# Plain fp32 products for 64 up blocks of a two-layer expert-retrieval kernel

## The chip, the cores and the metric

The kernel runs on one core of one Trainium2 chip. The metric is the device time of one execution in microseconds; smaller is better. Engines are named as in the profile: PE (matrix products; PEld its weight loads), DVE, ACT, POOL, and SP, which here only issues transfers.

## What is computed

A decoder trunk of two layers over 512 tokens of width 1024, in fp32. Layer 0 mixes tokens by sparse attention, layer 1 by a Mamba-2 scan; each adds a cross-attention into 256 memory tokens. After either mixer comes the part that the change touches, PEER: every token asks for experts by a product key, and each expert is one neuron.

```
q = (h @ w_q).reshape(b, s, 8, 2, 128)
scores = einsum('bshic,ikc->bshik', q, sub_keys)
top_s, top_i = top_k(scores, 16)
...
expert, gate = the best 16 of the 256 pairs, softmax
act = gelu(einsum('td,thkd->thk', xt, u[et]))
out = einsum('thk,thkd->td', act * gt, v[et])
```

There are 128 x 128 = 16384 experts, 8 heads and 16 experts a head, so a token uses 128 of them.

## The kernel before, in words

PE's fast product takes fp32r operands. To keep fp32 accuracy, `split` (L74 to L78) writes an operand as a sum hi + lo: ACT copies hi (L77), and DVE, or POOL by default in `wblock`, subtracts lo = src - hi (L78). `mm3` (L68 to L72) then makes three products: hi hi, hi lo, lo hi. The names w_raw, w_hi, w_lo are a weight block of 128x1024 and its parts; hT is the normed and transposed activation, hi and lo.

`peer` treats the four tiles of 128 tokens in two ways. Tile 0 is **gathered**: `gather_tile` fetches for each of the 128 slots one row of u, later one of v, for all 128 tokens (POOL's indirect transfers, L1087), and DVE multiplies and sums (L1093, L1104). Tiles 1 to 3, 384 tokens, are computed **densely** over all experts: an up block is 128 experts, `act = gelu(uT . hT)`, and a down block multiplies act with the gate matrix gt and adds `act^T . v` into six PSUM banks, acc. There are 128 up and 128 down blocks a layer.

The stages of a layer's `peer`:

- the norm with its transposes (`norm_T`, `transpose_o`), and the 16 w_q blocks with their scores (sc) and top-16 searches on DVE;
- for the tiles in the order 1, 2, 0, 3: `decode` (DVE), and for tiles 1 to 3 `gate_blocks`, which builds the gate matrices in 8 chunks of 16 tokens a tile: four DVE products of 128x2048 (tiles oh, L1067 to L1070), 32 PE products g (L1075), four ACT copies st (L1076). They go to DRAM (gd). Beside that the first SPILL = 32 up blocks run, whose act goes to DRAM too (ad);
- the 32 down blocks of the spilled blocks, with act_r read back;
- the ring: up block i and down block i - 8 in turn for the other 96 blocks, then the last 8 down blocks;
- the sums: x += acc for tiles 1 to 3 (L969), and for tile 0 the two halves of the gather's acc and x (L1106, L1107). Layer 1 is followed by the final norm.

RATE says how many rows of tile 0 are gathered for each down block: 0.7 in the spilled part, 2.75 in the ring, 1.1 at its end; 257 steps are needed. The order in which each engine's instructions stand is set by a scheduler when the program is built. It keeps the order of dependent work but moves independent work by its own estimates, within the pools' buffers: w_raw has 3, w_hi and w_lo 2, oh 9. An engine then keeps its order strictly. Buffers of the pool p_pre (the gates) and of p_v (down blocks and rows) share memory, so the second can be filled only as the first comes free.

Of the kernel before, what the change touches and what calls it, by code (L numbers as in the profile page):

```python
# [10 lines left out]
F32 = mybir.dt.float32  # L11
# [4 lines left out]
F16 = mybir.dt.float16  # L16
AF = mybir.ActivationFunctionType
# [5 lines left out]
D = 1024  # L23
S = 512
NT = 4
KC = D // 128
# [9 lines left out]
class Trunk:  # L36
# [116 lines left out]

    def norm_T(self, xs, x, hi, lo, parts=2):


        nc = self.nc
        with self.tc.high_priority(self.hp):
            for t, xt in enumerate(x):
                s = xs(t)  # L160
                r = self.tile_rstd(xt, s, parts)
                nc.vector.scalar_tensor_tensor(s, xt, r, self.grow, op0=OP.mult, op1=OP.mult)
                self.transpose_o(s, 0, KC, (hi, lo), t)

# [183 lines left out]

    def transpose_o(self, o, k0, k1, oT, t, k_src=None):

        nc = self.nc
        d = 0 if k_src is None else k_src - k0
        for k in range(k0, k1, 4):
            n = min(4, k1 - k)
            p = self.psum([128, 4, 128], "tr")
            for i in range(n):
                nc.tensor.transpose(p[:, i], o[:, (k + d + i) * 128:(k + d + i + 1) * 128], self.ident)
            sl = slice(t * 128, t * 128 + 128)
            self.split(oT[0][:, k:k + n, sl], oT[1][:, k:k + n, sl], p[:, :n])

    def out_proj(self, l, oT, order, banks):
# [467 lines left out]
    GS = 32768.0  # L829
    RATE = (0.7, 2.75, 1.1)  # L830

    def peer(self, l, banks):
        self.use_banks(tr=banks[:2], mm=banks[2:4], sc=banks[4:5], g=banks[6:])
        nc, tc, I = self.nc, self.tc, self.I
        ND = NT - 1
        NC = ND * 128 // self.CH
        ad = self.dram.tile([self.SPILL, 128, ND * 128], F32, name=f"ad{l}")
        gd = self.dram.tile([NC, 128, 128 * self.CH], F32, name=f"gd{l}")
        with ExitStack() as es:
            up = es.enter_context(tc.tile_pool(name="p_u", bufs=2))  # L840
            res = es.enter_context(tc.tile_pool(name="p_res", bufs=1))
            exi = res.tile([128, 128], I32, name="exi")
            gate0 = res.tile([128, 128], F32, name="gate0")
            h0 = res.tile([128, D], F32, name="h0")
            hT = self.hT
            with ExitStack() as e2:
                pre = e2.enter_context(tc.tile_pool(name="p_pre", bufs=1))
# [8 lines left out]
                nc.sync.dma_start(sk, I["sub_keys"][l])  # L856
                self.norm_T(lambda t: pre.tile([128, D], F32, tag="oh", name="xs", bufs=9) if t else h0,
                            [self.x[:, t] for t in range(NT)], hT[0], hT[1])
                self.load_gain(3 if l == 0 else 5)
# [20 lines left out]
                for t in self.ORDER:  # L880
                    e, g = self.decode(pre, iu[:, t], bv[:, t], bp[:, t])
                    if t:
                        self.gate_blocks(pre, e, g, gd, (t - 1) * 128 // self.CH)
                    else:
                        nc.vector.scalar_tensor_tensor(e[0], e[0], 128.0, e[1], op0=OP.mult, op1=OP.add)
                        nc.vector.tensor_copy(exi, e[0])
                        nc.vector.tensor_copy(gate0, g)
            vp = es.enter_context(tc.tile_pool(name="p_v", bufs=2))
            self.use_banks(acc0=banks[:2], acc1=banks[4:6], acc2=banks[6:], mm=banks[2:4],
                           up=banks[2:4] + banks[5:6])  # L890
            acc = [[self.psum([128, 512], f"acc{t}") for _ in range(2)] for t in range(ND)]
            G = self.gather_tile(l, vp, h0, exi, gate0)
            acts, last = {}, []

            def up_block(i):

                w = self.wblock(I["uT"][l, i], eng=nc.vector if i >= self.SPILL else None)
                p = self.psum([128, ND * 128], "mm" if i >= self.SPILL else "up")
                for k in range(KC):
                    self.mm3(p, (w[0][:, k], w[1][:, k]), (hT[0][:, k, 128:], hT[1][:, k, 128:]), k == 0, k == KC - 1)  # L900
                a = up.tile([128, ND * 128], F32, tag="act", name="act", bufs=self.RING)
                nc.scalar.activation(a, p, AF.Gelu)
                if i < self.SPILL:
                    nc.sync.dma_start(ad[i], a)
                else:
                    acts[i] = a

# [43 lines left out]

            for i in range(self.SPILL):
                up_block(i)
            for j in range(self.SPILL):
# [40 lines left out]
    def decode(self, pool, iu, bv, bp):  # L995


        nc = self.nc
# [14 lines left out]
        for i in range(2):  # L1013
# [6 lines left out]
            nc.vector.tensor_copy(rf, ru)  # L1020
            im = pool.tile(shp, F16, tag="oh", name="tk_im", bufs=9)
            nc.scalar.copy(im, ix4[:, :, i, :, None].to_broadcast(shp))
            oh = pool.tile(shp, F16, tag="oh", name="tk_oh", bufs=9)
            nc.vector.tensor_tensor(oh, rf[:, :, None, :].to_broadcast(shp),
# [17 lines left out]
    def gate_blocks(self, pool, e, gate, gd, c0):  # L1042
# [17 lines left out]
        for c in range(128 // B):  # L1060
# [3 lines left out]
            col = [sT[:, i, c * B:(c + 1) * B, None].to_broadcast(shp) for i in range(4)]  # L1064
            oh = [pool.tile([128, B, 128], F16, tag="oh", name="oh", bufs=9) for i in range(4)]
            o4 = [x.rearrange("p t (a b) -> p t a b", b=2) for x in oh]
# [142 lines left out]
```

## Time and profile before

| | before |
|---|---|
| median of 3 runs (lowest to highest) | 3251.77 us (3250.94 to 3254.98) |
| the profiled execution | 3256.72 us |
| its span, first to last instruction | 3254.9 us |
| mean granted PE clock | 0.971 of full speed |
| busy: PE, DVE, ACT, POOL | 3013.9, 2374.3, 1362.3, 1212.0 us |

A view with starts gives us from the span's start, then the duration. A line number such as L78 can be that of a helper, so the tile's name tells what it works on. A matmul's duration is longer than its step, since products are pipelined; the pace is read from one start to the next. What stands in brackets behind a row is how long the engine had been idle, and what released it. The granted clock is a share of 2.4 GHz.

### The profile page before, as it was taken

The numbers are of one execution on the slowest core, as the hardware profiler recorded it, in microseconds if no ns is written. First come the engines' busy times: TensorE is split into PE (matmuls) and PEld (weight loads), VectorE is DVE, ScalarE is ACT, GpSimd is POOL, SyncE is SP. The second block draws the span as 40 slices with busy tenths as digits, with TensorE's granted clock in tenths as the row PEclk, the third lists the DMA queues.
The fourth block names the chain that finished last, engine by engine and source line by source line (L and its number), as shares of the span: only waits on it lengthen the run. The fifth ranks groups of instructions, "written<-read, shape, count | busy, mean of one in ns | idle before, by whom it ended". The sixth has DMA issues, their size and how long they took to land.

```text
span 3254.9 us, 44982 instructions
## 1 busy us (share of the span) xinstructions
PE 3013.9 (93%) x16369; PEld 2671.7 (82%) x16374; DVE 2374.3 (73%) x4611; ACT 1362.3 (42%) x2053; POOL 1212.0 (37%) x763
## 2 busy tenths in 40 slices
PE   8899987778999999999999999778889999999998
PEld 7787776777899999999978777667679999999997
DVE  6964898836587777877767579885566777777775
ACT  5573346643333333333345533665323333333332
POOL 3212435431044345554213334445112434445540
PEclk9899999999999999999999999889999999999999
DMA  4211224488699989998521122455877999989982
GB/s 164 90 50 54 74 99 185 184 292 292 222 329 335 322 316 324 336 324 315 201 93 52 67 72 83 181 187 214 310 256 270 318 326 335 323 313 327 332 290 82
DMA packets 241495, 727.33 MB, mean 223 GB/s; under 512 B 22092, under 2 KB 92792, under 8 KB 238200
## 3 DMA queue, kind: packets, MB, share of 16 engines
q1 hardware_dynamic: 162288, 448.66, 38.4%
q0 software_dynamic: 73728, 268.47, 23.7%
q10 hardware_dynamic: 5256, 7.32, 0.8%
q8 instruction: 128, 2.10, 0.3%
q14 instruction: 95, 0.78, 0.1%
HBM read 658.29 MB, written 66.08 MB: 223 GB/s over the span
## 4 chain that ended last, share of the span: by engine, by line
PE 73%; DVE 12%; DMA 5%; ACT 5%; issue 4%; POOL 2%; SPq 0%; POOLq 0%; DVEq 0%; ACTq 0%
PE mm L70 11%; PE mm L72 11%; PE mm L71 11%; PE acc L71 10%; PE acc L70 10%; PE acc L72 10%; DMA act_r<-ad 4%; ACT st L1076 2%; POOL w_lo L78 1%; PE g L1075 1%; PE up L70 1%; PE up L72 1%; PE up L71 1%; DVE oh L1070 1%; ACT w_hi L77 1%
## 5 line engine op out<-in xcount | busy, mean ns | idle before, releaser
L77 ACT CAST w_hi<-w_raw 128x1024 fp32r<-128x1024 f32 (+2 forms) x353 | 366.1, 1037 | 777.5 <-PE mm L71 609.0
L72 PE MATMUL mm<-hT,w_lo 128*128 128x384 f32 (+2 forms) x1928 | 668.1, 347 | 9.2 <-POOL w_lo L78 9.2
L70 PE MATMUL mm<-hT,w_hi 128*128 128x384 f32 (+2 forms) x1928 | 669.0, 347 | 0.0
L78 POOL TENSOR_TENSOR w_lo<-w_raw,w_hi 128x1024 fp32r<-128x1024 f32 (+2 forms) x157 | 472.0, 3014 | 528.4 <-ACT w_hi L77 464.0
L71 PE MATMUL mm<-hT,w_hi 128*128 128x384 f32 (+2 forms) x1928 | 667.8, 346 | 0.0
L71 PE MATMUL acc<-v_lo,a_hi 128*128 128x512 f32 x1536 | 608.2, 396 | 36.0 <-DVE v_lo L78 36.0
L70 PE MATMUL acc<-v_hi,a_hi 128*128 128x512 f32 x1536 | 605.1, 394 | 9.4 <-ACT a_hi L77 9.4
L72 PE MATMUL acc<-v_hi,a_lo 128*128 128x512 f32 x1536 | 603.6, 393 | 0.0
L1087 POOL DMA_INDIRECT row<-in_u,exi x256 | 300.0, 1172 | 697.1 <-DVE junk L1093 687.8
L1087 POOL DMA_INDIRECT row<-in_v,exi x256 | 386.5, 1510 | 391.0 <-DVE acc L1104 302.0
L78 DVE TENSOR_TENSOR w_lo<-w_raw,w_hi 128x1024 fp32r<-128x1024 f32 (+1 forms) x196 | 240.1, 1225 | 388.8 <-ACT w_hi L77 388.8
L72 PEld LDWEIGHTS mm<-hT,w_lo 128*128 128x128 f32 x1928 | 364.2, 189 | 25.1 <-POOL w_lo L78 12.7
L70 PEld LDWEIGHTS mm<-hT,w_hi 128*128 128x128 f32 x1928 | 365.3, 190 | 21.0 <-ACT hT L77 0.4
L71 PEld LDWEIGHTS mm<-hT,w_hi 128*128 128x128 f32 x1928 | 364.5, 189 | 20.3 <-DVE hT L78 0.4
L78 DVE TENSOR_TENSOR v_lo<-v_raw,v_hi 128x1024 fp32r<-128x1024 f32 x256 | 312.4, 1220 | 90.3 <-ACT v_hi L77 89.5
L71 PEld LDWEIGHTS acc<-v_lo,a_hi 128*128 128x128 f32 x1536 | 292.2, 190 | 97.0 <-DVE v_lo L78 42.7
L70 PEld LDWEIGHTS acc<-v_hi,a_hi 128*128 128x128 f32 x1536 | 291.8, 190 | 68.0 <-ACT a_hi L77 10.4
L72 PEld LDWEIGHTS acc<-v_hi,a_lo 128*128 128x128 f32 x1536 | 292.1, 190 | 62.5 <-DVE a_lo L78 0.3
L1104 DVE SCALAR_TENSOR_TENSOR acc<-row,gact,acc 128x1024 f32<-128x1024 f32 x252 | 314.5, 1278 | 0.0
L1093 DVE SCALAR_TENSOR_TENSOR junk<-row,h 128x1024 bf16<-128x1024 f32 x256 | 311.6, 1217 | 0.5 <-DMA row<-in_u,exi 0.4
L77 ACT CAST a_hi<-act 128x384 fp32r<-128x384 f32 x192 | 98.8, 514 | 495.2 <-PE acc L71 484.4
L77 ACT CAST v_hi<-v_raw 128x1024 fp32r<-128x1024 f32 x256 | 268.0, 1047 | 30.5 <-DMA v_raw<-in_v 19.1
(352 smaller groups left out, 4543.4 us busy)
## 6 DMA issues: line engine op xcount, KB each, us to landing
w_raw<-in_uT SPq DMA_DIRECT2D x256, 512.0 KB
v_raw<-in_v SPq DMA_DIRECT2D x256, 512.0 KB
gd<-st SPq DMA_DIRECT2D x24, 2048.0 KB
gt<-gd SPq DMA_DIRECT2D x32, 1536.0 KB
w_raw<-in_w_q SPq DMA_DIRECT2D x32, 512.0 KB
ad<-act SPq DMA_DIRECT2D x64, 192.0 KB
act_r<-ad SPq DMA_DIRECT2D x64, 192.0 KB
w_raw<-in_w_o SPq DMA_DIRECT2D x16, 512.0 KB
```

Of the source, the lines that this page charges most:

```text
L70: mm(out, lhs[0], rhs[0], start=start, stop=False)
L71: mm(out, lhs[0], rhs[1], start=False, stop=False)
L72: mm(out, lhs[1], rhs[0], start=False, stop=stop)
L77: self.nc.scalar.copy(hi, src)
L78: return (eng or self.nc.vector).tensor_tensor(lo, src, hi.bitcast(F32), OP.subtract)
L1070: nc.vector.tensor_tensor(o4[2], o4[0], col[2], OP.mult)
L1075: nc.tensor.matmul(p[:, i], oh[1][:, q + i], oh[k][:, q + i], start=k == 2, stop=k == 3)
L1076: nc.scalar.mul(st[:, :, o + q:o + q + 4].rearrange("p i t -> p t i"), p, 1.0 / self.GS)
L1087: nc.gpsimd.indirect_dma_start(out=g, out_offset=None, in_=I[name], in_offset=bass.IndirectOffsetOnAxis(ap=exi[:, s:s + 1], axis=0))
L1093: nc.vector.scalar_tensor_tensor(j, g, 1.0, h, op0=OP.mult, op1=OP.mult, accum_out=act[:, s:s + 1])
L1104: nc.vector.scalar_tensor_tensor(a, g, act[:, s:s + 1], a, op0=OP.mult, op1=OP.add)
```

## The change

The 32 up blocks beside the gates take the raw weights and an unsplit fp32 copy hw of the normed, transposed tiles 1 to 3, and PE makes one plain fp32 product for each of a block's eight 128-row slices. hw is written by ACT in `transpose_o` from the same PSUM tile as hT. hw and the blocks' act_s lie in p_pre, oh goes from 9 buffers to 8, and the pool p_u of the ring's act is opened after p_pre is closed, not before. RATE becomes (0.6, 2.6, 1.1).

```diff
-    def transpose_o(self, o, k0, k1, oT, t, k_src=None):
+    def transpose_o(self, o, k0, k1, oT, t, k_src=None, whole=None):
...
             self.split(oT[0][:, k:k + n, sl], oT[1][:, k:k + n, sl], p[:, :n])
+            if whole is not None:
+                nc.scalar.copy(whole[:, k:k + n, t * 128 - 128:t * 128], p[:, :n])
...
-    RATE = (0.7, 2.75, 1.1)
+    RATE = (0.6, 2.6, 1.1)
...
-            up = es.enter_context(tc.tile_pool(name="p_u", bufs=2))
...
+                hw = pre.tile([128, KC, ND * 128], F32, name="hw")
+                self.norm_T(lambda t: pre.tile([128, D], F32, tag="oh", name="xs", bufs=8) if t else h0,
+                            [self.x[:, t] for t in range(NT)], hT[0], hT[1], whole=hw)
...
+                self.use_banks(up=banks[2:4] + banks[5:6])
+                for i in range(self.SPILL):
+                    w = self.wst.tile([128, 1072], F32, tag="w_raw", name="w_raw", bufs=3)[:, :D]
+                    w = w.rearrange("p (k c) -> p k c", k=KC)
+                    nc.sync.dma_start(w, I["uT"][l, i])
+                    p = self.psum([128, ND * 128], "up")
+                    for k in range(KC):
+                        nc.tensor.matmul(p, w[:, k], hw[:, k], start=k == 0, stop=k == KC - 1)
+                    a = pre.tile([128, ND * 128], F32, tag="act_s", name="act_s", bufs=3)
+                    nc.scalar.activation(a, p, AF.Gelu)
+                    nc.sync.dma_start(ad[i], a)
+            up = es.enter_context(tc.tile_pool(name="p_u", bufs=2))
...
             def up_block(i):
-
-                w = self.wblock(I["uT"][l, i], eng=nc.vector if i >= self.SPILL else None)
-                p = self.psum([128, ND * 128], "mm" if i >= self.SPILL else "up")
+                w = self.wblock(I["uT"][l, i], eng=nc.vector)
+                p = self.psum([128, ND * 128], "mm")
...
-            for i in range(self.SPILL):
-                up_block(i)
             for j in range(self.SPILL):
                 rows(down_block(j), self.RATE[0])
```

How the built order moves, at three places. First ACT beside the first gate chunks of layer 0, before:

```order
L1076 ACTIVATE st<-g 128x4x128 x8
L77 CAST w_hi<-w_raw 128x1024
L902 ACTIVATE act<-up 128x384
L1076 ACTIVATE st<-g 128x4x128 x4
L77 CAST w_hi<-w_raw 128x1024
L1076 ACTIVATE st<-g 128x4x128 x2
```

and now (line numbers of the changed file are larger by 7 here; act_s is the spilled block's act, tk_im a copy that `decode` needs):

```order
L900 ACTIVATE act_s<-up 128x384
L1083 ACTIVATE st<-g 128x4x128 x8
L900 ACTIVATE act_s<-up 128x384
L1083 ACTIVATE st<-g 128x4x128 x8
L1029 COPY tk_im<-tk_ix 128x2048 x2
L1083 ACTIVATE st<-g 128x4x128 x2
```

The w_hi casts are gone, a Gelu stands between two chunks, and both tk_im copies stand ahead of a tile's last four st. On PE 39 up products now stand ahead of the first gate product, and one or three (some 2.7 on average) between the halves and the chunks of a tile; 15 stand between tiles 1 and 2, and 29 between tiles 2 and 3.

Second PE, where the gates of layer 0 end. Before, 139 split up products followed the last gate product, and then the down blocks:

```order
L71 MATMUL up<-hT_88,w_hi 128x384
L72 MATMUL up<-hT_87,w_lo 128x384
L70 MATMUL acc_6067<-v_hi,a_hi 128x512
L71 MATMUL acc_6067<-v_lo,a_hi 128x512
L72 MATMUL acc_6067<-v_hi,a_lo 128x512
```

Now 87 plain ones follow it, and then products of the ring's up blocks (84 until the first acc):

```order
L1082 MATMUL g<-oh 128x128
L898 MATMUL up<-hw,w_raw 128x384 x87
L70 MATMUL mm<-hT_87,w_hi 128x384
L71 MATMUL mm<-hT_88,w_hi 128x384
L72 MATMUL mm<-hT_87,w_lo 128x384
```

The ring's products that stood behind the 576 spilled down products become 132 instead of 216.

Third DVE, at the end of layer 1. Before, the last v_lo is followed by the sums of tiles 1 to 3 alone:

```order
L78 TENSOR_TENSOR v_lo<-v_raw,v_hi 128x1024
L969 TENSOR_TENSOR x<-acc_19866,x 128x512
L969 TENSOR_TENSOR x<-acc_19867,x 128x512
L969 TENSOR_TENSOR x<-acc_19868,x 128x512
L149 SCALAR_TENSOR_TENSOR w_raw,nss<-x 128x512
```

and now the gather's last step and its sums come among them (L1113 and L1114 are the old L1106 and L1107, L976 the old L969):

```order
L1111 SCALAR_TENSOR_TENSOR acc<-row,gact,acc 128x1024
L976 TENSOR_TENSOR x<-acc_19688,x 128x512
L1113 TENSOR_TENSOR acc<-acc 128x1024
L976 TENSOR_TENSOR x<-acc_19689,x 128x512
L1114 TENSOR_TENSOR x<-x,acc 128x1024
L976 TENSOR_TENSOR x<-acc_19690,x 128x512
```

Tile 0's norm, which stood far ahead of the last down blocks, comes last of the four. On SP's queue the loads of gt and v stood between the last ad stores; now they come behind all of them.

## Rows read from the trace of the kernel before

**Rows 1.** The page, busy us, share of the span and instructions of each engine.

```profile
PE 3013.9 (93%) x16369; PEld 2671.7 (82%) x16374; DVE 2374.3 (73%) x4611; ACT 1362.3 (42%) x2053; POOL 1212.0 (37%) x763
```

**Rows 2.** Stretches: length, busy PE, PEld, DVE, ACT, POOL, clock, DMA share, GB/s.

```profile
431.80:704.30 272.50, 209.72 (x1554) 192.61 (x1552) 202.84 (x324) 166.39 (x190) 135.49 (x39) 0.91 0.51 187
704.30:866.00 161.70, 139.25 (x576) 111.50 (x577) 99.12 (x143) 50.18 (x69) 22.38 (x22) 0.96 0.84 290
866.00:1663.00 797.00, 797.00 (x4042) 726.83 (x4041) 605.30 (x749) 281.92 (x393) 322.02 (x233) 1.00 0.83 294
```

**Rows 3.** Waits from 431.8 to 704.3: total us, times, longest.

```profile
PE up L72 <- POOL w_lo L78: 30.6, 9, 7.7
...
DVE oh L1069 <- PE g L1075: 28.7, 5, 9.0
```

**Rows 4.** Groups from 430 to 720: busy us, mean ns of one, idle before.

```profile
L78 POOL TENSOR_TENSOR w_lo<-w_raw,w_hi 128x1024 fp32r<-128x1024 f32 x32 | 130.5, 4088 | 125.6 <-ACT w_hi L77 103.5 <-PE up L72 15.1 <-PE g L1075 6.9
...
L1022 ACT COPY tk_im<-tk_ix 128x2048 f16<-128x2048 f16 x8 | 15.0, 1907 | 7.9 <-DVE tk_ix L1001 7.9
```

**Rows 5.** Timeline of DVE and POOL beside the gates: start, us, operation.

```profile
458.08 3.45 DVE L1024 TENSOR_TENSOR tk_oh<-tk_rf,iorank 128x2048 f16<-128x2048 f16 x1
...
471.06 3.42 DVE L1070 TENSOR_TENSOR oh<-oh,sT 128x2048 f16<-128x2048 f16 x1
...
487.07 19.11 POOL L78 TENSOR_TENSOR w_lo<-w_raw,w_hi 128x1024 fp32r<-128x1024 f32 x2 [9.21 <-ACT w_hi L77]
...
510.20 1.23 DVE L1069 TENSOR_TENSOR oh<-oh,sT 128x2048 f16<-128x2048 f16 x1 [8.55 <-PE g L1075]
```

**Rows 6.** Timeline of PE: the first gate product, and one chunk.

```profile
474.53 1.05 PE L1075 MATMUL g<-oh 128*128 128x128 f16 x16 [1.15 <-DVE oh L1070]
...
639.59 1.07 PE L1075 MATMUL g<-oh 128*128 128x128 f16 x16
640.47 0.42 PE L72 MATMUL up<-hT,w_lo 128*128 128x384 f32 x1
641.37 0.61 PE L1075 MATMUL g<-oh 128*128 128x128 f16 x8 [0.48 <-ACT st L1076]
...
642.69 0.42 PE L70 MATMUL up<-hT,w_hi 128*128 128x384 f32 x1
642.95 0.33 PE L71 MATMUL up<-hT,w_hi 128*128 128x384 f32 x1
643.12 0.34 PE L72 MATMUL up<-hT,w_lo 128*128 128x384 f32 x1
```

**Rows 7.** Timeline of PE in layer 1: two plain fp32 products.

```profile
1752.95 0.81 PE L790 MATMUL mm<-state,ccT 128*128 128x384 f32 x2
1753.60 0.81 PE L799 MATMUL mm<-xe,btm 128*128 128x384 f32 x2
```

**Rows 8.** Timeline of SP's issues, DVE and PE where the gates end.

```profile
688.70 0.37 SPq L912 DMA_DIRECT2D gt<-gd  x1
...
696.95 0.44 SPq L917 DMA_DIRECT2D act_r<-ad  x1
...
706.96 0.56 DVE L925 TENSOR_TENSOR act_r<-act_r,gt 128x384 f32<-128x384 f32 x1 [1.17 <-DMA act_r<-ad]
...
708.12 0.80 PE L70 MATMUL acc<-v_hi,a_hi 128*128 128x512 f32 x1 [3.87 <-ACT a_hi L77]
```

**Rows 9.** Waits from 704.3 to 866.

```profile
DVE act_r L925 <- DMA act_r<-ad: 47.1, 22, 6.9
...
PE acc L71 <- DVE v_lo L78: 18.6, 8, 5.2
```

**Rows 10.** Timeline of ACT in the norm of layer 0.

```profile
317.25 0.59 ACT L77 CAST hT<-tr 128x512 fp32r<-128x512 f32 x1 [4.98 <-PE tr L357]
```

**Rows 11.** Timeline of DVE near the end of layer 0's down blocks.

```profile
1595.61 1.22 DVE L1107 TENSOR_TENSOR x<-x,acc 128x1024 f32<-128x1024 f32 x1
...
1613.66 1.28 DVE L162 SCALAR_TENSOR_TENSOR w_raw<-x,rs_r,grow 128x1024 f32<-128x1024 f32 x1
```

More of the change, by code (lines that the diff above doesn't have):

```diff
@@ L152, in tile_rstd, with norm_T @@
         return self.rstd(ss[:, 0:1], D, 1)
-    def norm_T(self, xs, x, hi, lo, parts=2):
+    def norm_T(self, xs, x, hi, lo, parts=2, whole=None):
         nc = self.nc
@@ L162, in norm_T @@
                 nc.vector.scalar_tensor_tensor(s, xt, r, self.grow, op0=OP.mult, op1=OP.mult)
-                self.transpose_o(s, 0, KC, (hi, lo), t)
+                self.transpose_o(s, 0, KC, (hi, lo), t, whole=whole if t else None)
     def wblock(self, src, shape=(128, KC, 128), eng=None):
@@ L856, in peer @@
                 nc.sync.dma_start(sk, I["sub_keys"][l])
-                self.norm_T(lambda t: pre.tile([128, D], F32, tag="oh", name="xs", bufs=9) if t else h0,
-                            [self.x[:, t] for t in range(NT)], hT[0], hT[1])
+                hw = pre.tile([128, KC, ND * 128], F32, name="hw")
+                self.norm_T(lambda t: pre.tile([128, D], F32, tag="oh", name="xs", bufs=8) if t else h0,
+                            [self.x[:, t] for t in range(NT)], hT[0], hT[1], whole=hw)
                 self.load_gain(3 if l == 0 else 5)
@@ L887, in peer @@
                         nc.vector.tensor_copy(gate0, g)
+                self.use_banks(up=banks[2:4] + banks[5:6])
[10 more added lines that the diff above has]
+            up = es.enter_context(tc.tile_pool(name="p_u", bufs=2))
             vp = es.enter_context(tc.tile_pool(name="p_v", bufs=2))
-            self.use_banks(acc0=banks[:2], acc1=banks[4:6], acc2=banks[6:], mm=banks[2:4],
-                           up=banks[2:4] + banks[5:6])
+            self.use_banks(acc0=banks[:2], acc1=banks[4:6], acc2=banks[6:], mm=banks[2:4])
             acc = [[self.psum([128, 512], f"acc{t}") for _ in range(2)] for t in range(ND)]
@@ L895, in up_block @@
             def up_block(i):
-                w = self.wblock(I["uT"][l, i], eng=nc.vector if i >= self.SPILL else None)
-                p = self.psum([128, ND * 128], "mm" if i >= self.SPILL else "up")
+                w = self.wblock(I["uT"][l, i], eng=nc.vector)
+                p = self.psum([128, ND * 128], "mm")
                 for k in range(KC):
                     self.mm3(p, (w[0][:, k], w[1][:, k]), (hT[0][:, k, 128:], hT[1][:, k, 128:]), k == 0, k == KC - 1)
[L901 to L906, printed above, removed]
+                acts[i] = up.tile([128, ND * 128], F32, tag="act", name="act", bufs=self.RING)
+                nc.scalar.activation(acts[i], p, AF.Gelu)
             def down_block(j):
@@ L1020, in decode @@
             nc.vector.tensor_copy(rf, ru)
-            im = pool.tile(shp, F16, tag="oh", name="tk_im", bufs=9)
+            im = pool.tile(shp, F16, tag="oh", name="tk_im", bufs=8)
             nc.scalar.copy(im, ix4[:, :, i, :, None].to_broadcast(shp))
-            oh = pool.tile(shp, F16, tag="oh", name="tk_oh", bufs=9)
+            oh = pool.tile(shp, F16, tag="oh", name="tk_oh", bufs=8)
             nc.vector.tensor_tensor(oh, rf[:, :, None, :].to_broadcast(shp),
@@ L1064, in gate_blocks @@
             col = [sT[:, i, c * B:(c + 1) * B, None].to_broadcast(shp) for i in range(4)]
-            oh = [pool.tile([128, B, 128], F16, tag="oh", name="oh", bufs=9) for i in range(4)]
+            oh = [pool.tile([128, B, 128], F16, tag="oh", name="oh", bufs=8) for i in range(4)]
             o4 = [x.rearrange("p t (a b) -> p t a b", b=2) for x in oh]
```

## The prediction

> **What bounds the kernel now.** I began with the busy shares. PE is busy for 93% of the span, DVE for 73%, POOL for 37% [rows 1]. Such a share is an average over stages with different limits, so the table of stretches comes next [rows 2]. From 866 to 1663 PE is busy for 797.00 of 797.00 us at clock 1.00: there only fewer products could save time, and the change leaves those products as they are. Two other stretches are looser. From 431.8 to 704.3 the gate matrices and the 32 spilled up blocks run side by side: PE 209.7 of 272.5 us at clock 0.91, DVE 202.8. From 704.3 to 866 the 32 spilled down blocks run. Layer 1 runs the same code with other weights, so I take its saving alike.
>
> In the first stretch the waits tell who ends last [rows 3]: PE waited 30.6 us for POOL's w_lo, DVE 28.7 us for PE's gate products. POOL's w_lo takes 4088 ns on average [rows 4]; two in succession took 19.11 us, between 487.07 and 506.2, while DVE ran its fp16 products without a gap, and DVE then stood 8.55 us until PE had come past the late weights [rows 5]. It works the other way as well: an L1024 of DVE took 3.45 us and an L1070 3.42 us beside a w_lo on POOL, where the same size takes 1.23 us undisturbed [rows 5]. So POOL's splitting holds up PE and DVE, and the engines wait in a ring.
>
> **What the change removes.** Per layer 32 w_hi on ACT, 32 w_lo on POOL and 768 products of 384 columns at 0.174 us, the step from 642.95 to 643.12 [rows 6]: 24 a block, 4.2 us. POOL is left with nothing in this stage, so both kinds of hold-up go.
>
> **What it adds, on PE.** 256 plain fp32 products of 384 columns. Two such products stand back to back in the Mamba layer: L790 starts at 1752.95 and L799 at 1753.60, each in two passes [rows 7]. So one costs 0.65 us, a block 5.2 us against 4.2: 256 x 0.65 = 166.4 us instead of 133.6. The Trainium skill, "TensorE: Matmul & The Clock Gate", section Back-to-back issue gap, gives N/2.4 + 2.5 ns: for two passes of 768 that is an estimate of 0.645 us, and the stage would be 1.3 us shorter a layer. By the same rule one of the old products would take 162.5 ns; the row has 174, and the row decides.
>
> **The new stage, by PE's order.** PE keeps its written order, so I add up that order from 431.8.
> - 24 gate chunks. A chunk from its first product at 639.59 to the next up product at 642.69 takes 3.1 us, of which the waits for ACT's st are part [rows 6]. In the new order one fp32 product stands inside each chunk, where 0.9 us are free (640.47 to 641.37), so 24 of the 256 cost nothing as long as st sets the pace. 24 x 3.1 = 74.4.
> - The other 232 products: 232 x 0.65 = 150.8.
> - The four score products of 128 columns, a third of 0.65 each: 1.
> - The start: after 39 up products PE is ready at 458.2. The first gate product came at 474.5 before [rows 6]. Three DVE operations that POOL held up by 2.2 us each lie before it (two of them in [rows 5]), so it can now come at 467.9: 9.7 us of waiting.
> - ACT's two tk_im copies ahead of the last st of a tile (1.9 us each [rows 4]) delay the last chunk by about 2.5 us, twice: 5. Gelu between two st, some 12 times 0.2: 2.
>
> Together 242.9, so the last up product ends at about 675 instead of 704.25 (708.12 less the 3.87 of waiting [rows 8]): **30 us a layer saved**. DVE does not hold this up. Undisturbed, a chunk is four operations of 1.2 us there, 4.9 at most, against PE's 3.1 + 2.7 x 0.65 = 4.9 on average. With 8 oh buffers instead of 9 a chunk's second product (not its third) waits for PE, and DVE has some 3 us in hand; I cost it at nothing, and if it fails it costs about 0.4 us a chunk, 10 us a layer.
>
> **Handing over.** Before, PE stood 3.87 us between the last up and the first acc product [rows 8]. gt was issued at 688.70, act_r at 696.95, and the first multiplication started at 706.96: 10 us behind act_r, 18 behind gt. Now gt, v and act_r all come behind the last ad store, about 3 us after the end, so the first acc product can come 15 to 22 us after it. In between stand 84 ring products that came later before: 84 x 0.174 = 14.7 us. I take 3 us idle, as against 3.9: -1. If the cover is gone, the price is 8.
>
> **Down blocks.** 576 products of 512 columns, at 512/384 of 0.174 = 0.23 us, are 132.5 us; the stretch took 161.7 [rows 2]. PE waited 18.6 us there for v_lo, DVE 47.1 us for act_r [rows 9]. RATE takes 3 of 22 gathered rows away, 1.6 MB, and some two ring weights are loaded earlier: 2.6 MB of 47, at 290 GB/s 9 us of transfer. The bounds are 0 (what is late is one load, not the sum) and -9; I take **-4 a layer**. The Trainium skill, "SBUF — State Buffer", section A bandwidth-pool intuition that's wrong, gives a core some 358 GB/s of HBM: by that the 47 MB need an estimated 131 us, less than PE's 132.5, and the saving would be 0. No row here shows that ceiling; the mean of 290 [rows 2] stands below it.
>
> **The copy hw.** Six ACT copies of 128x512 a layer; the alike hT cast takes 0.59 us [rows 10]. They stand between casts for which PE waits, but ACT has pauses there. +1 a layer, bounds 0 and 3.5.
>
> **The ends of the layers.** With RATE 2.6 the gathering lasts until the last down block. Before, its sums (1.22 us each) were done at 1596.8 and tile 0's norm at 1614.9, both beside the down products [rows 11]. Now they stand between and behind the last x additions on DVE. In layer 1 two sums of 1.2, a square over half a tile (half a sum: 0.6), a norm of 1.28 and small steps come on top of DVE's closing work, less about 1 us that PE's last products cover: +5. In layer 0 tile 0's transposes and 24 short products that filled PE at the change of layers come later: +4. Bounds +3 and +7 each.
>
> **Sum.** 2 x (-30 - 1 - 4 + 1) + 9 = -59 us. The profiled execution took 3256.7 us, 1.8 outside its span of 3254.9; it lies 4.9 above the median of the runs, 3251.8. So 3251.8 - 59 = 3192.8, rounded to **3193 us**.
>
> **Rivals.**
> - *More*: nothing waits in the new stage. Then PE needs 166.4 + 24 x 1.76 (16 gate products in 0.88 us [rows 6]) + 1 = 209.6 us, 33 less than I count: 3193 - 2 x 33 = 3127. For it: POOL is out. Against it: the st of ACT remain, and the first gate matrix has to wait for DVE's decoding.
> - *Less*: a chunk takes 3.6 us instead of 3.1 (an ACT step of some 0.5 us between two st, an estimate from st's steps of 0.9 [rows 6]), 12 us a layer, the hand-over costs 4 more, and fewer rows give nothing: 3193 + 2 x 20 = 3233. For it: act_r was the late load throughout [rows 9].
> - *Slower*: the clock. The plain fp32 products of [rows 7] stand two in a row among split products, at full pace. Now 87 fp32 products stand in a row. If PE were granted the lower of its two levels (1.2 instead of 2.4 GHz) in them, each would take 1.3 us: 87 x 0.65 = 56.6 more a layer, 3193 + 113 = 3306. It decides from about 45 such products a layer (2 x 45 x 0.65 = 59). Against it: the stage's mean of 0.91 came with waits of up to 7.7 us [rows 3], and the new order has fewer.
> - *It does not overlap*: PE waits for raw weights, since SP's queue holds them behind gd and ad stores. The order issues a weight two blocks, 10 us, ahead; I give it little. If the 145 products between first and last gate matrix (232 less 87) lost half their cover, some 47 us a layer: 3193 + 94 = 3287.
>
> **How the numbers follow.** Forecast 0.70, with a range of its own from 3166 to 3214; more 0.06; less 0.17; the clock 0.05; no overlap 0.02. A measurement here can tell a difference from about 0.2%, 6.5 us. Forecast, more and nearly all of less are faster by more than that: 0.91. Same 0.03, out of the weaker end of less; slower 0.06. The range of 8 in 10 runs from 3162 to 3230: it takes in the forecast's own bounds and the nearer half of less, and leaves out more and the clock.
>
> **What would show it.** Right: no PE wait on POOL in the stage, 0.65 us from one up product to the next, DVE's 128x2048 products all at 1.22 us, the last up near 675, the first acc some 17 us behind it. The layers' ends about 4 us longer. Wrong: a granted clock near 0.5 in the row of 87, chunks of over 5.5 us, or a first acc over 23 us behind the last up.

## The result: 51.6 us faster, and the profile after

The changed kernel takes **3200.31 us** (median of 4 runs, 3199.93 to 3203.8), the kernel before 3251.86. The ratio is 0.9842, 95% interval 0.9825 to 0.9859. The forecast was 3193 us, in a range from 3162 to 3230. The profiled execution took 3199.93 us, with a span of 3198.1; it lies 56.8 us under the profiled one of before, for which the sum of the forecast was -59.

The page of the changed kernel, busy us, share of the span and instructions of the engines, against [rows 1]:

```profile
PE 3042.7 (95%) x15862; PEld 2570.8 (80%) x15862; DVE 2303.8 (72%) x4611; ACT 1305.1 (41%) x2001; POOL 953.0 (30%) x699
```

PE is busy 29 us longer with 507 instructions fewer, in a span that is 57 us shorter. POOL lost 259 us. Where the time went is read from the stretches between the same events as in [rows 2]: first up product, last up product, first acc product, first ring product behind the spilled down blocks, last acc product of layer 0, first z product of layer 1 (z is a product of its mixer), and the end. From the last up to the first acc product is called the hand-over here; the second stretch of [rows 2] held it, 3.8 us, together with 157.9 us of spilled down blocks. Stretches of the changed kernel: length, busy PE, PEld, DVE, ACT, POOL, clock, DMA share, GB/s.

```profile
431.80:669.57 237.77, 221.69 (x1299) 141.25 (x1297) 168.73 (x325) 137.17 (x161) 1.13 (x2) 0.99 0.56 203
669.57:689.52 19.95, 15.13 (x87) 14.71 (x85) 4.88 (x5) 5.91 (x9) 5.82 (x5) 1.00 0.90 305
689.52:846.06 156.54, 143.05 (x576) 114.85 (x577) 95.38 (x139) 47.59 (x66) 18.70 (x19) 0.92 0.80 278
846.06:1627.35 781.29, 781.29 (x3949) 711.24 (x3947) 597.38 (x727) 274.47 (x380) 322.35 (x234) 1.00 0.85 300
1627.35:1654.37 27.02, 19.11 (x129) 18.30 (x129) 17.76 (x51) 10.81 (x21) 2.90 (x7) 0.81 0.35 104
...
2245.14:2397.28 152.14, 139.95 (x577) 112.70 (x578) 94.90 (x139) 47.57 (x66) 19.81 (x19) 0.94 0.82 284
...
3178.54:3198.10 19.56, 0.15 (x1) 0.00 (x0) 11.61 (x39) 1.74 (x6) 3.73 (x4) 0.57 0.26 107
```

And the stretch of the kernel before that answers to the end of layer 0:

```profile
1662.90:1678.82 15.92, 15.14 (x122) 14.49 (x121) 11.65 (x32) 8.26 (x15) 1.40 (x5) 1.00 0.57 177
```

Set against each other, in us, layer 0 and layer 1 (changes from before to after; in brackets the lengths):

| step | forecast per layer | layer 0 | layer 1 |
|---|---|---|---|
| first to last up product | -30 | -34.7 (272.5 to 237.8) | -33.4 (272.5 to 239.1) |
| last up to first acc, less 84 products of 0.176 moved there | -1 | +1.3 (3.9 to 19.95) | +0.1 (5.6 to 20.5) |
| spilled down blocks | -4 | -1.4 (157.9 to 156.5) | -7.7 (159.8 to 152.1) |
| ring, less the same 84 products | 0 | -0.8 | +0.1 |
| the copy hw | +1 | 0.0 | +1.2 |
| end of the layer | +4, +5 | +11.1 (15.9 to 27.0) | +7.3 (12.3 to 19.6) |

The columns add up to -24.5 and -32.4, or -56.9. **The gate stage** gave 8 us more than forecast, **the ends** took 9.4 us more.

In the gate stage PE no longer waits for POOL. Ahead of the first gate product, at 466.9, it stands 7.0 us for DVE's decoding. What is left of its waits from there on, in us, times, longest:

```profile
PE g L1082 <- ACT st L1083: 8.4, 26, 0.8
```

That answers to 30.6 us on POOL's w_lo in [rows 3]. A chunk on PE, and the run of plain fp32 products behind the gates (one row: start, us, operation, count of passes):

```profile
476.45 1.06 PE L1082 MATMUL g<-oh 128*128 128x128 f16 x16
477.35 0.86 PE L898 MATMUL up<-hw,w_raw 128*128 128x384 f32 x2
478.24 0.61 PE L1082 MATMUL g<-oh 128*128 128x128 f16 x8
...
479.57 2.15 PE L898 MATMUL up<-hw,w_raw 128*128 128x384 f32 x6
...
614.07 55.63 PE L898 MATMUL up<-hw,w_raw 128*128 128x384 f32 x172
```

From 476.45 to 479.57 a chunk takes 3.1 us, as forecast. In the last row 172 passes lie in 55.63 us; one pass alone takes 0.486, so the step is (55.63 - 0.49) / 171 = 0.3225 us, or 0.645 for a product. The stretch of that run shows the clock, at 1.00 throughout:

```profile
613.86:669.57 55.71, 55.71 (x175) 32.79 (x174) 1.23 (x1) 8.06 (x14) 0.00 (x0) 1.00 0.54 181
```

The prediction's estimate of 0.645, worked out from the formula in the Trainium skill, "TensorE: Matmul & The Clock Gate", section Back-to-back issue gap, agrees with it; the 768 columns a pass were put in by the prediction, that section does not give them.

DVE's groups beside the gates, in the changed kernel and in the one before (busy us, mean ns of one, idle before):

```profile
L1075 DVE TENSOR_TENSOR oh<-iokey,sT 128x2048 f16<-128x2048 f16 x24 | 29.3, 1220 | 0.2
```

```profile
L1070 DVE TENSOR_TENSOR oh<-oh,sT 128x2048 f16<-128x2048 f16 x24 | 35.8, 1490 | 0.0
```

The mean of 1490 ns was a mixture of 1.22 us and some of up to 3.4; now the means of all four oh operations are 1219 or 1220 ns, and of the 28.7 us in which DVE waited for gate products [rows 3] 0.9 is left.

### The profile page after: what moved, and what is told of

It reads as the page before. It is cut to its first block, busy times and chain, and to the rows that moved or that the text cites. A ratio compares the mean times of both kernels' runs of the same rounds, so it can differ in the third digit from the quotient of the medians.

```text
span 3198.1 us, 43835 instructions
## 1 busy us (share of the span) xinstructions
PE 3042.7 (95%) x15862; PEld 2570.8 (80%) x15862; DVE 2303.8 (72%) x4611; ACT 1305.1 (41%) x2001; POOL 953.0 (30%) x699
## 4 chain that ended last, share of the span: by engine, by line
PE 75%; DVE 12%; DMA 5%; ACT 5%; issue 2%; POOL 1%; SPq 0%; POOLq 0%; ACTq 0%; DVEq 0%
PE acc L71 10%; PE acc L70 10%; PE acc L72 10%; PE mm L70 10%; PE mm L71 10%; PE mm L72 10%; PE up L898 8%; DMA act_r<-ad 3%; ACT st L1083 3%; PE g L1082 1%; DVE tk_s L982 1%; DMA gt<-gd 1%; DVE tki L985 1%; DVE tki L984 1%; PE po L597 1%
## 5 line engine op out<-in xcount | busy, mean ns | idle before, releaser
L77 ACT CAST w_hi<-w_raw 128x1024 fp32r<-128x1024 f32 (+2 forms) x289 | 298.7, 1034 | 712.8 <-PE mm L71 599.5
L70 PEld LDWEIGHTS mm<-hT,w_hi 128*128 128x128 f32 x1928 | 364.5, 189 | 22.1 <-ACT hT L77 1.4
L898 PE MATMUL up<-hw,w_raw 128*128 128x384 f32 x1024 | 358.1, 496 | 0.0
L1100 DVE SCALAR_TENSOR_TENSOR junk<-row,h 128x1024 bf16<-128x1024 f32 x256 | 312.0, 1219 | 2.1 <-DMA row<-in_u,exi 2.0
L78 POOL TENSOR_TENSOR w_lo<-w_raw,w_hi 128x1024 fp32r<-128x1024 f32 (+3 forms) x93 | 213.0, 2299 | 265.4 <-ACT w_hi L77 245.2
```

The lines of the kernel that those rows point to most:

```text
L70: mm(out, lhs[0], rhs[0], start=start, stop=False)
L77: self.nc.scalar.copy(hi, src)
L78: return (eng or self.nc.vector).tensor_tensor(lo, src, hi.bitcast(F32), OP.subtract)
L898: nc.tensor.matmul(p, w[:, k], hw[:, k], start=k == 0, stop=k == KC - 1)
L1100: nc.vector.scalar_tensor_tensor(j, g, 1.0, h, op0=OP.mult, op1=OP.mult, accum_out=act[:, s:s + 1])
```

## The hand-over and the end of a layer in the trace after

The hand-over in layer 0, in SP's issues, then DVE and PE:

```profile
670.63 0.33 SPq L901 DMA_DIRECT2D ad<-act_s  x1
...
674.38 0.38 SPq L921 DMA_DIRECT2D gt<-gd  x1
...
675.66 1.04 SPq L926 DMA_DIRECT2D act_r<-ad  x1
```

```profile
688.32 0.56 DVE L934 TENSOR_TENSOR act_r<-act_r,gt 128x384 f32<-128x384 f32 x1 [7.75 <-DMA v_raw<-in_v]
```

```profile
689.52 0.57 PE L70 MATMUL acc<-v_hi,a_hi 128*128 128x512 f32 x1 [4.82 <-issue]
```

act_r is issued 5 us behind the last store and the first multiplication starts 12.7 us later, so the first acc product comes 20 us behind the last up product. The 84 ring products that stand between them keep PE busy for 15.1 of these. DVE and ACT stand for the loads here, and PE once those products are done, while the DMA engines are nearly full: share 0.90 and 305 GB/s in the stretch.

The end of layer 0, on PE and on DVE:

```profile
1627.12 0.39 PE L72 MATMUL acc<-v_hi,a_lo 128*128 128x512 f32 x1
1633.58 1.94 PE L357 MATMUL tr<-ident,w_raw 128*128 128x128 f32 x8 [6.08 <-DVE rs_t L94]
```

```profile
1623.31 1.22 DVE L1113 TENSOR_TENSOR acc<-acc 128x1024 f32<-128x1024 f32 x1
...
1632.16 1.28 DVE L162 SCALAR_TENSOR_TENSOR w_raw<-x,rs_r,grow 128x1024 f32<-128x1024 f32 x1
```

The sums L1113 and L1114 stand among the last x additions now; the norm of tile 0, L162, is done at 1633.4, where it was done at 1614.9 before, 48 us ahead of the end of the down products [rows 11]. PE, which found tile 0 ready in the kernel before, stands 6.08 us here and 1.80 four microseconds later. What follows is slower too: the stretch from the first transpose on, two short products in it, and two such products of the kernel before.

```profile
1633.58:1640.00 6.42, 4.62 (x21) 4.11 (x21) 6.16 (x11) 3.33 (x6) 0.00 (x0) 0.50 0.04 14
```

```profile
1641.04 0.43 PE L72 MATMUL mm<-w_hi,hT 128*128 128x268 f32 x1
1641.26 0.42 PE L70 MATMUL mm<-w_hi,hT 128*128 128x268 f32 x1
```

```profile
1663.02 0.29 PE L71 MATMUL mm<-w_lo,hT 128*128 128x268 f32 x1
1663.15 0.28 PE L72 MATMUL mm<-w_hi,hT 128*128 128x268 f32 x1
```

They step by 0.22 us instead of 0.13. The stretch from 1627.35 to 1654.37 has a mean clock of 0.81, against 1.00 before: after it had stood, PE ran at the lower of its two levels, 0.50 from 1633.58 to 1640. Of the 11.1 us, 7.1 are idle time (7.9 against 0.8) and 4.0 are busy time (19.1 against 15.1), of which tile 0's eight transposes, which lay in the ring before, are some 1.8 at this clock.

The end of layer 1 is another case, since no PE product follows there: of its 7.3 us 5.4 are DVE's, busy for 11.6 us behind the last acc product instead of 6.25, and the rest is standing in the chain of the last norm.

## The experiments

Theory: POOL's splitting and DVE's fp16 products hold each other up, PE waits for both, and the change frees all three. Rivals: the gain comes from the blocks' new place in the program, or only from PE's own wait for w_lo. A second question was what the new rates do, a third what the plain fp32 products cost where nothing hides them.

**Split again, at the new place.** In the loop over spilled blocks; the copy hw goes as well:

```
-  nc.sync.dma_start(w, I["uT"][l, i])
+  w = self.wblock(I["uT"][l, i])
...
   for k in range(KC):
-      nc.tensor.matmul(p, w[:, k], hw[:, k], start=k == 0, stop=k == KC - 1)
+      self.mm3(p, (w[0][:, k], w[1][:, k]), (hT[0][:, k, 128:], hT[1][:, k, 128:]), k == 0, k == KC - 1)
```

> The changed kernel with split up blocks again: w_hi on ACT, w_lo on POOL, three products, no copy hw; place, pools, 8 oh buffers and rates as in the change. Theory (POOL's splitting holds up DVE and PE): the stage from 431.8 goes back to about 272 us, so the last up product ends near 704 instead of 669.6, and the time is about 3200 + 2 x 33 = 3266 us, 3255 to 3275. Rival (the gain came from the place of the blocks in the program and their pools): the stage stays under 250 us, 3200 to 3224 us.

Measured: 3261.58 us, ratio to the kernel before 1.0019 (1.0009 to 1.0029). The stage, and PE's and DVE's waits in it:

```profile
428.70:697.80 269.10, 205.85 (x1555) 188.53 (x1554) 204.11 (x325) 166.85 (x192) 125.64 (x34) 0.92 0.50 180
```

```profile
PE up L72 <- POOL w_lo L78: 30.1, 9, 6.6
DVE oh L1072 <- PE g L1079: 28.3, 5, 9.0
```

Both waits are back as they were in [rows 3], and the stage is 31 us longer than in the changed kernel, 29 in layer 1. It is 3.4 us shorter than in the kernel before, so the new place, the pools and the eighth oh buffer can be the source of 3 to 4 us of the gain there, no more. The rest sits in the way the blocks are computed.

**POOL alone.** Behind each gelu a subtraction on POOL that nobody reads.

```
-  nc.scalar.activation(a, p, AF.Gelu)
+  nc.scalar.activation(a, p, AF.Gelu, accum_out=pace[:, i:i + 1])
   nc.sync.dma_start(ad[i], a)
+  lo = self.wst.tile([128, 1072], F32R, tag="w_lo", name="w_lo", bufs=2)[:, :D]
+  nc.gpsimd.tensor_tensor(lo.rearrange("p (k c) -> p k c", k=KC), hw[:, :, :128],
+                          pace[:, i:i + 1, None].to_broadcast([128, KC, 128]), OP.subtract)
```

> The changed kernel, and behind each of the 32 gelus a subtraction of 128x1024 on POOL whose result nobody reads (it writes a w_lo buffer, as POOL did before). PE waits for nothing new. Theory A (POOL and DVE hold each other up): DVE's 128x2048 fp16 products go from 1.22 us on average to 1.6 or more, POOL's subtractions to about 4 us, and the stage grows by 15 to 40 us a layer: about 3250 us, 3230 to 3280. Theory B (what was saved is PE's own wait for the late w_lo): DVE's products may slow, the stage grows by less than 4 us a layer, 3200 to 3208 us.

Measured: 3248.73 us, ratio 0.9984 (0.9974 to 0.9994): 48 us of the 51.6 are gone again by the medians, 46 by the ratios. The stage in layer 0, PE's waits for DVE, DVE's and POOL's groups in it, and a piece of POOL's and DVE's timelines:

```profile
430.60:691.20 260.60, 229.17 (x1300) 144.00 (x1298) 196.55 (x325) 139.87 (x192) 111.98 (x33) 0.95 0.51 183
```

```profile
PE tr L1058 <- DVE tk_e L1041: 19.0, 3, 10.4
...
PE g L1086 <- DVE oh L1081: 3.2, 4, 1.1
```

```profile
L1079 DVE TENSOR_TENSOR oh<-iokey,sT 128x2048 f16<-128x2048 f16 x24 | 32.6, 1357 | 0.0
```

```profile
L904 POOL TENSOR_TENSOR w_lo<-hw,pace 128x1024 fp32r<-128x1024 f32 x32 | 112.8, 3532 | 137.5 <-ACT act_s L901 137.5
```

```profile
468.20 2.53 POOL L904 TENSOR_TENSOR w_lo<-hw,pace 128x1024 fp32r<-128x1024 f32 x1 [10.57 <-ACT act_s L901]
473.76 2.07 POOL L904 TENSOR_TENSOR w_lo<-hw,pace 128x1024 fp32r<-128x1024 f32 x1 [3.03 <-ACT act_s L901]
...
486.48 19.57 POOL L904 TENSOR_TENSOR w_lo<-hw,pace 128x1024 fp32r<-128x1024 f32 x1 [10.65 <-ACT act_s L901]
...
506.00 1.89 POOL L904 TENSOR_TENSOR w_lo<-hw,pace 128x1024 fp32r<-128x1024 f32 x1
```

```profile
468.89 2.92 DVE L1078 TENSOR_TENSOR oh<-iokey,sT 128x2048 f16<-128x2048 f16 x1
...
474.00 2.91 DVE L1081 TENSOR_TENSOR oh<-oh,sT 128x2048 f16<-128x2048 f16 x1
```

The stage is 23 us longer than in the changed kernel, 21 in layer 1, though no engine reads what POOL makes; theory B, with less than 4, falls. DVE is busy 196.6 us instead of 168.7 with as many instructions, and the mean of 1357 ns falls short of the 1.6 us that were expected. PE feels it through DVE: it stands 31.4 us instead of 16.1, and what is new are the waits for DVE's decoding (19.0 instead of 7.0) and for its oh (3.2 instead of none). The other 7.5 us are busy time, 229.2 instead of 221.7, at a mean clock of 0.95 instead of 0.99. The edit also puts 31 short readings of a sum on ACT, 0.2 us each; PE's wait for ACT's st is as it was, 8.5 us against 8.4.

The timelines show the lock itself: the two subtractions that start at 468.20 and 473.76 take some 2 us, and the DVE product beside each takes 2.9 instead of 1.22. The one that starts at 486.48 takes 19.57 us, while DVE, up to 504.07, starts an fp16 product every 1.13 us; the next takes 1.89 again. The Trainium skill, "SBUF — State Buffer", section 🔬 SBUF: two separate sides, says that DVE and GpSimd share one pair of ports, and that whoever has it keeps it for a whole instruction while the other one waits. The short subtractions agree with that; the long one waited through some fifteen instructions of DVE, not one, and why it did not get in between two of them, as the others did, no run here shows.

So 21 to 23 us come from POOL's mere presence in this stage. Splitting costs 29 to 31; the difference is not taken apart by a run. With the blocks split again PE stands 63.3 us and is busy for 205.9, 47 more of standing and 16 less of work than in the changed kernel; 30.1 of the standing are waits for w_lo, which itself is late through the lock. Outside the stage the hand-over is some 3 us longer than in the changed kernel. DVE's first w_lo of the ring waits 3.9 us there for POOL's unread buffer, but the run with the old rates below has 22.1 us of hand-over in layer 0 without it, so the cause is open.

**The rates.** Three runs: the changed kernel with the old rates, with a middle one, and the kernel before with the new ones.

```
-  RATE = (0.6, 2.6, 1.1)
+  RATE = (0.7, 2.75, 1.1)
```

> The changed kernel with RATE back at (0.7, 2.75, 1.1). In the changed kernel the two layer ends cost 11.1 and 7.3 us more than before. Theory (the gathered rows end too late): with the old rates the last row comes some 11 blocks earlier, the sums and the norm of tile 0 lie beside the down products again, and both ends fall back to before's 15.9 us (last acc product to first z product) and 12.3 us (last acc product to the end): -18.4. The spilled down phase gets its three rows back and loses up to 4 us a layer: about 3186 us, 3182 to 3192. Rival (the ends are longer for another reason, the clock or the new pools): the ends stay at 27 and 19.6 us, and the time is 3200 to 3208 us.

```
-  RATE = (0.6, 2.6, 1.1)
+  RATE = (0.6, 2.7, 1.1)
```

> The changed kernel with RATE (0.6, 2.7, 1.1): 19 rows in the spilled down phase as now, then 2.7 instead of 2.6 a block. Theory: 32 x 0.6 + 88 x 2.7 = 256.8, so the last row comes 8 down blocks before the end; both layer ends fall back to about 16 and 12 us, nothing else moves: 3200 - 18 = 3182 us, 3179 to 3187. Rival (the ring has no room for more rows, its DMA share is 0.85 at 300 GB/s): 9 rows more of 0.5 MB before the ring's end at 300 GB/s are 15 us a layer of PE waiting, and the time is 3200 to 3212 us.

And in the kernel before:

```
-  RATE = (0.7, 2.75, 1.1)
+  RATE = (0.6, 2.6, 1.1)
```

> The kernel before with only RATE changed to (0.6, 2.6, 1.1). Theory (these rates only move the gathering behind the last down block): both layer ends get longer by about 11 and 7 us, the spilled down phase gains nothing: about 3252 + 17 = 3269 us, 3262 to 3274. Rival (my term of -4 us a layer in the down phase is right, and the ends cost what I forecast, 9): 3252 + 1 = 3253 us.

Measured: 3184.85 us (ratio 0.9781, 0.9765 to 0.9798) with the old rates, 3185.21 us (0.9789, 0.9773 to 0.9806) with the middle one, 3263.72 us (1.0024, 1.0013 to 1.0035) for the kernel before with the new rates. The end of layer 0 and the spilled down blocks with the old rates, and its sum and norm of tile 0 on DVE:

```profile
1629.70:1645.60 15.90, 15.12 (x121) 14.48 (x120) 11.61 (x31) 8.19 (x15) 1.38 (x5) 1.00 0.57 177
691.90:847.40 155.50, 140.64 (x576) 112.87 (x577) 98.51 (x145) 47.55 (x66) 21.68 (x22) 0.94 0.84 282
```

```profile
1560.75 1.22 DVE L1113 TENSOR_TENSOR acc<-acc 128x1024 f32<-128x1024 f32 x1
...
1580.41 1.29 DVE L162 SCALAR_TENSOR_TENSOR w_raw<-x,rs_r,grow 128x1024 f32<-128x1024 f32 x1
```

And the kernel before with the new rates, the same two stretches in layer 0 and the very end:

```profile
706.40:858.80 152.40, 140.14 (x577) 112.11 (x578) 93.25 (x135) 48.92 (x66) 19.24 (x19) 0.95 0.84 286
1654.70:1682.50 27.80, 19.92 (x129) 19.09 (x129) 17.90 (x51) 10.86 (x21) 2.86 (x7) 0.75 0.34 102
...
3241.60:3261.50 19.90, 0.20 (x1) 0.00 (x0) 11.66 (x39) 1.80 (x6) 3.74 (x4) 0.58 0.26 105
```

The ends follow the rates, whatever computes the up blocks: 27 to 28 and 20 us with the new ones, 16 and 12 with the old ones, and in layer 0 the lower clock comes and goes with the gap. With the norm of tile 0 done at 1581.7, PE has the next layer's first transposes at hand when the down blocks end. The down phase says less: 155.5 and 155.2 us with all 22 rows in the changed kernel, 156.5 and 152.1 with 19; in the kernel before 152.4 and 155.3 with 19, against 157.9 and 159.8 with 22. So fewer rows are worth some 5 us a layer there in the kernel before, and in the changed kernel nothing that can be told from its scatter. The kernel before became 8 us slower with them (against the 3255.35 us that it took beside this run), not 17: its ends cost 19.5, and the down phase, which was expected to gain nothing, gives 10 back. The middle rate gains 15, not 18: in layer 0 the ring is 3.7 us longer, with one wait of 2.6 us of a transpose for a norm, that of tile 0, which comes late inside the ring there.

**One oh buffer fewer**, at each of the oh tags, as here:

```
-  oh = [pool.tile([128, B, 128], F16, tag="oh", name="oh", bufs=8) for i in range(4)]
+  oh = [pool.tile([128, B, 128], F16, tag="oh", name="oh", bufs=7) for i in range(4)]
```

> The changed kernel with 7 oh buffers instead of 8. Theory (PE's order sets the pace of a chunk, about 5 us, and DVE has some 0.3 to 1 us in hand in each): the ninth buffer that the change took cost nothing, and the eighth costs 0 to 0.3 us a chunk: 3200 to 3214 us. Rival (DVE was held by the buffers already): 0.4 us a chunk or more for each buffer, 24 chunks, two layers, 3220 us or more; then the change lost as much with the ninth.

The edit also takes one buffer of eight each from two tiles of layer 1's scan, dec and cde. Measured: 3199.49 us, ratio 0.9832 (0.9815 to 0.9848), the same as with 8. So the eighth costs nothing. That the ninth cost nothing is not run, but fits: with 8 buffers DVE waits only 0.9 us for gate products in the stage.

**The expensive end of the gate stage.** First, the last 10 of the 32 blocks split again (the branch for i < 22 is the plain fp32 form as it is), with the middle rate:

```
+  if i < 22:
...
+  else:
+      w = self.wblock(I["uT"][l, i], eng=nc.vector)
+      for k in range(KC):
+          self.mm3(p, (w[0][:, k], w[1][:, k]), (hT[0][:, k, 128:], hT[1][:, k, 128:]), k == 0, k == KC - 1)
```

> The changed kernel with RATE (0.6, 2.7, 1.1), and of the 32 spilled up blocks only the first 22 as plain fp32 products; the last 10, which PE does alone behind the last gate product, are split again, with w_lo on DVE. Theory (behind the gates nothing hides a product, so there the price on PE counts): 80 x 0.627 = 50.2 us become 240 x 0.174 = 41.8, 8.4 less a layer; against 3185 us with the same rates that is 3168 us, 3164 to 3174. Rival (PE waits for w_hi and w_lo there, or DVE's splitting comes ahead of the last gate matrices): the stage is not shorter, 3182 to 3195 us.

Measured: 3170.96 us, ratio 0.9744 (0.9728 to 0.976). The 0.627 us in this and the next expectations is too low; with the measured 0.645 the saving is 80 x 0.645 - 41.8 = 9.8 a layer. From the first to the last up product it was 10.0 and 9.5 us against the run with the same rates (238.1 and 239.4 to 228.1 and 229.9). The stretch behind the gates, which answers to the 55.71 us above:

```profile
614.60:659.50 44.90, 44.90 (x251) 43.58 (x250) 12.26 (x10) 15.37 (x22) 0.00 (x0) 1.00 0.63 221
```

PE is busy throughout: neither ACT's nor DVE's part of the split is waited for there. The total gained 14 us instead of the 19.6 by this price: the hand-over of layer 1, the down blocks of layer 0, and its ring and end taken together are some 2 us longer each in this execution, for which these runs show no cause.

Then fewer spilled blocks, the rest going to the ring as split ones:

```
-  SPILL = 32            RATE = (0.6, 2.6, 1.1)
+  SPILL = 24            RATE = (0.6, 2.55, 1.1)
```

> The changed kernel with 24 spilled blocks instead of 32 and RATE (0.6, 2.55, 1.1), which ends the gathering 8 down blocks before the end. Theory: the run of 87 up products behind the gates shrinks to 23, 64 x 0.627 = 40.1 us less in the gate stage; 8 blocks more in the ring cost 8 x 24 x 0.174 = 33.4; and 8 of 32 down blocks leave the phase that waits for loads (153 to 157 us for 132.5 us of products), some 5 us. Per layer -12: about 3185 - 24 = 3161 us, 3155 to 3172. Rival (the ring, at a DMA share of 0.85, has no room for 8 blocks' splitting and 6 rows more): PE waits there, 3180 to 3210 us.

```
+  SPILL = 21            RATE = (0.6, 2.5, 1.1)
```

> The changed kernel with 21 spilled blocks and RATE (0.6, 2.5, 1.1). Its up products end with the last gate chunk, none stands behind it. Theory (only blocks behind the gates are too dear): against 24 blocks 23 products x 0.627 = 14.4 us and the last chunks' gaps go from PE's stage, 3 x 24 x 0.174 = 12.5 us come into the ring, and three blocks leave the waiting phase, some 2 us: 4 us less a layer, about 3149 us, 3142 to 3156. Rival (the hand-over gets uncovered, since the gate matrices' last store is now right ahead of the first down blocks): the idle time ahead of the first acc product rises from about 5 us to 10 or more: 3157 to 3175 us.

```
+  SPILL = 16            RATE = (0.6, 2.4, 1.1)
```

> The changed kernel with 16 spilled blocks and RATE (0.6, 2.4, 1.1): the last tile's gate matrices have no up product beside them. Theory (inside the gate stage a product is free only as long as DVE's four operations of 1.14 us a chunk are slower than PE): the last 8 chunks run at DVE's pace, some 4.6 us instead of 5.0, so of the 41 products (25.7 us) that leave the inside of the stage only about 5 us are won, 14.4 behind the gates and some 5 in the down phase as well, and 8 x 24 x 0.174 = 33.4 us come into the ring: 9 us more a layer than with 24 blocks, about 3157 + 18 = 3175 us, 3163 to 3185. Rival (PE is the bound inside the gate stage too, so that a product costs 0.627 us wherever it stands): 3157 - 2 x (40.1 + 5 - 33.4) = 3134 us.

Measured: 3157.17 us with 24 blocks (ratio 0.9704, 0.9687 to 0.972), **3146.44 us with 21** (0.9669, 0.9653 to 0.9685), 3182.31 us with 16 (0.978, 0.9764 to 0.9797). The best of them is 54 us, 1.7%, faster than the change, and 3.3% faster than the kernel before; 15 of the 54 are what the middle rate alone gave, since in these three runs too the gathering ends before the layer does. From the first gate product to the last, in the changed kernel and with 16 blocks, and a wait of PE in the latter:

```profile
466.89:613.86 146.97, 137.87 (x1036) 92.07 (x1035) 133.77 (x166) 114.44 (x130) 0.00 (x0) 1.00 0.63 240
```

```profile
468.20:613.50 145.30, 123.33 (x1001) 88.09 (x999) 138.16 (x170) 116.13 (x129) 0.00 (x0) 0.98 0.60 230
```

```profile
PE g L1082 <- DVE oh L1077: 7.2, 7, 1.3
```

The stretch is only 1.7 us shorter with 16 blocks than with 32, though PE has 14.5 us less to do in it. The up products that are gone stood just ahead of the last tile's chunks and between them; without them PE waits there for DVE, whose fp16 products then set the pace. So beside the last tile's gates the up products were as good as free; for the tiles ahead of it, where no run took any out, that is inferred. Behind the gates they are not free, and 11 of the 32 blocks stood there. With 21 blocks PE stands 4.17 us ahead of the first acc product, no longer than before, so the rival of that run (an uncovered hand-over) falls:

```profile
638.52 0.77 PE L70 MATMUL acc<-v_hi,a_hi 128*128 128x512 f32 x1 [4.17 <-issue]
```

With 16 the rival by which PE is the bound inside falls as well; the run came out 7 us above what the theory gave, with PE waiting in layer 0 9.0 us for an activation of the ring at the hand-over and 6.2 for the first acc product, so that the hand-over is filled less well there.

## Why the prediction was right, and which terms were off

- **What bounds.** Right. POOL's splitting held the stage: split blocks at the new place bring 29 to 31 us of the 33 to 35 back, and POOL alone, with as many instructions as it had before, 21 to 23. One reading was coarse: of the two w_lo that took 19.11 us "in succession" the first took 16.78, while DVE's products ran, and the second 2.37.
- **The price of a plain fp32 product.** 0.65 forecast, 0.645 measured over 172 passes.
- **The new stage by PE's order.** 242.9 us forecast, 237.8 and 239.1 measured. The chunk of 3.1 us and the first gate product (467.9 forecast, 466.9 measured) held. The 5 us for ACT's two tk_im copies were no time of their own: three up products stand inside the chunk that waits for them, not one, so PE works meanwhile, and its longest wait for st in the stage is 0.8 us. With the 0.005 us on 232 products that takes 6 us off the sum, 1 to 2 more than the stage shows. That DVE does not hold the stage up held: PE's list of waits has no oh. But it was close, since with up products taken from the last tile PE waits for DVE at once and the stretch to the last gate product shrinks by 1.7 us only.
- **The clock.** 1.00 in the run of 87 products. That rival is out, as is the one by which raw weights come late: from the first gate product on PE's list of waits has st alone.
- **The hand-over.** First acc product 20 us behind the last up product, forecast 17 and at most 22; idle 4.8 and 5.3 instead of 3. The DMA engines are at a share of 0.90 there; that the loads are late for that reason is not shown.
- **Down blocks.** The mechanism is not borne out for the changed kernel: taking three rows out is worth nothing there that the run with the old rates could show, though some 5 us a layer in the kernel before. The -1.4 and -7.7 have no cause that these runs separate; the stretch scatters between 152 and 157 us over the variants with 32 blocks in the new place. That they add up to -9.1, near the forecast -8, is luck. The 161.7 us from which the term was taken also held 3.8 us of hand-over. The estimate by the Trainium skill, "SBUF — State Buffer", section A bandwidth-pool intuition that's wrong, some 358 GB/s for a core, made the saving 0; the 278 to 286 GB/s in these stretches stand well below that, so the 0 of the changed kernel is not shown to come from there.
- **The copy hw.** +1 a layer forecast, 0.0 and +1.2 measured; but the first up product of layer 0 comes between 429.3 and 433.0 us in the runs that have the copy, so no run sizes this term.
- **The ends of the layers.** This is the step that was mis-sized most: +4 and +5, with bounds of 3 and 7, became +11.1 and +7.3, and the forecast sign of "about 4 us longer" did not come. For layer 0 I had counted the late instructions on DVE, but not that the first transposes of the next layer wait for the whole chain through the norm of tile 0 (7.1 us more of standing), nor that the products behind the gap run at a lower granted clock. In layer 1 DVE's extra work was 5.4 us, near the forecast; the waits in its last norm were left out.
- **The reference point.** The sum of -59 was set against the median of before; against its profiled execution, 4.9 us slower than that median, -56.8 came out. So the errors of -8 in the gate stage and +9 in the ends cancel, which is luck, and most of the 2 us left is the hand-over. Some 5 of the 7 us between 3193 and 3200 come from setting rows of a slower execution against the median.

## What to carry to other kernels

A computation that takes an operand as it is can win though it costs the bottleneck engine more, if the preparation it saves runs on an engine that holds up another; look for that in the longest instructions of either, since the means hide it. Then ask for each piece whether it is hidden: an expensive form belongs only where another engine sets the pace, and the cheap form everywhere else (21 blocks, not 32). And background work that ends with the last instruction of a stage should end some blocks earlier, because what follows starts with its result.

## What the runs showed of the hardware

- A POOL subtraction of 128x1024 took 19.57 us while DVE ran fp16 products of 1.22 us without a pause, and others 2 to 2.5 us when they got in between two such products; the DVE product beside them then took 2.9 us.
- One plain fp32 product of 384 columns steps by 0.645 us, three split ones by 3 x 0.174 = 0.52 [rows 6]. Splitting is the cheaper form on PE, by 0.12 us a product, as long as somebody else's splitting is free.
- A row of 172 fp32 passes without a gap ran at clock 1.00; a stop of 6.08 us was followed by a stretch of 6.42 us, transposes and short products with gaps, at 0.50.
- The DMA engines moved 342 GB/s on average in the hand-over of the run with POOL's extra work, more than in any down phase of the runs with 32 blocks (272 to 288 GB/s), so those are not the most that they move:

```profile
691.20:713.80 22.60, 15.23 (x86) 14.64 (x85) 4.88 (x5) 5.96 (x9) 7.22 (x6) 0.96 0.96 342
```
